# Attention: the second batch of score maxima moved between the first four and the last two value tiles of a group

## The chip, the cores and the metric

The kernel runs on one core of one Trainium2 chip. The metric is the device time of one execution in microseconds; three executions of the kernel before are at hand.

## What is computed

One transformer layer over 2048 latent tokens with 256 context tokens as a prefix. The change touches attention alone:

```python
def attend(q, k, v):
    s = jnp.einsum('bkgqd,bknd->bkgqn', q, k, preferred_element_type=jnp.float32)
    p = jax.nn.softmax(s, axis=-1).astype(v.dtype)
    return jnp.einsum('bkgqn,bknd->bkgqd', p, v)
```

There are 8 query heads of 64 channels on 2 key heads, and 2048 + 256 = 2304 keys, that is 18 key tiles of 128. Everything is float32. The rest of the layer (projections, a gated MLP branch, the merge, a feed-forward network) comes before and behind it.

## The kernel before

Attention (`attend`, L1121) goes through 16 **units**. A unit (class `Unit`, L1993) is one block of 512 queries for two heads. It works in the transposed form: a score tile has 128 keys on the partitions and 512 queries along a row, so the softmax maximum of a query must be known before the scores are exponentiated. It is found in a separate pass, ahead of time, for a later unit:

- `maxima(n)` (L2022) takes the next n steps of 18. A step is two matmuls of 64 rows (one for each head, in the two halves of the array) into two PSUM banks, and two reductions on VectorE (DVE) out of them (L2048; the two steps on the context keys use L2043).
- `reference()` (L2052) joins a unit's maxima, `leading()` (L2059) transposes them and puts them by DMA into one row of the second score operand, so that the second score matmul subtracts them.

The unit itself handles its 18 key tiles in three **groups** of six (`GROUP`). For every tile, `first(j)` (L2077) and `second(j)` (L2087) issue two score matmuls each (L2082 and L2101) into two banks, and ScalarE (ACT) exponentiates both (L2105) into an SBUF tile. `values(j)` (L2108) multiplies the exponentials with the values (L2115); those of a group run one group later, from the list `pend`. A value tile is four matmul instructions of 64 columns, in two pairs. `values` also adds the exponentials of one tile to a running total for the softmax sums: on DVE for tiles 4, 8 and 14 (tile 2 only starts that total; L2128), on GpSimd (POOL) for the others (L2131). `leave()` (L2135) copies the finished output of a unit from its bank (ACT, L2138) and stores it by a DMA that ACT issues; it stands at the end of `pend` for the third group.

So TensorE's order in a group is: 24 score matmuls, a first batch of three maxima steps (6 matmuls; 10 instructions where the context keys are in it), 24 value matmuls of the group before, a second batch of three maxima steps. In the third group the two sums of an older unit (`sums`, L2153: L2157 on TensorE, the copy L2163 and two DMA issues on ACT) follow the values. In the first two groups the maxima are those of the next unit, in the third group those of the one after. At the end of the middle group `reference` of the next unit and `join` (L2141, DVE) of the unit before run, at the end of the third `remainder` (L2017, DVE). In units 1 to 4 a piece of `mod_part` (L355) runs at the fifth tile of a group: two DVE operations on weights and, now and then, a matmul.

All of this shares the eight PSUM banks (tag "b", L1122). One of them holds a unit's output from its first value tile, in the middle group, until `leave` has copied it. The exponentials lie in 8 buffers "p2" (tiles 0 to 3 of a group) and 8 buffers "t4" (tiles 4 and 5).

What sets the order: within `attend`, TensorE and DVE run in the order in which the program is written, because `attend` notes its range in `fixed` (L1170) and `order` (L1867) chains those two engines; new tiles of one tag are also first written in program order on every engine:

```python
            held = idx in pinned or (idx in fixed and i.engine in engines)
            held = held or (idx in loads and i.engine == self.nc.sync.engine)
            after = keys + ([i.engine] if held else [])
```

ACT, POOL and the DMA queue are ordered by the framework's scheduler.

Of the kernel before, what the change touches and what calls it, by code (L numbers as in the profile page):

```python
# [63 lines left out]
}  # L64
SLOTS = {tag: n for tags in POOLS.values() for tag, n in tags.items()}
GROUP = 6
ON_VECTOR = (2, 4, 8, 14)
LAST_ON_VECTOR = (2, 4, 7, 8, 9, 13, 14, 15)


class Kern:
# [1048 lines left out]
    def attend(self, units, late, mod):  # L1120
        self.psum({"b": 8})  # L1121
        begin = self.here()  # L1122
        pend = []
        for i, u in enumerate(units):
            at = lambda n: units[n] if 0 <= n < len(units) else None
            nxt, far, old, older = at(i + 1), at(i + 2), at(i - 1), at(i - 2)
            for gi, g in enumerate(range(0, NKT, GROUP)):
                group = range(g, g + GROUP)
                step = nxt if gi < 2 else far
                for j in group:  # L1130
                    u.first(j)
                    u.second(j)
                    if j % GROUP == 2 and far and gi == 0:
                        far.load()
                    if j % GROUP == 4 and nxt and gi == 2:
                        nxt.leading()
                    if not nxt:
                        next(late, None)
                    elif i and j % GROUP == 4:
                        next(mod, None)  # L1140
                if step:
                    step.maxima(3)
                for f in pend:
                    f()
                if gi == 1 and far:
                    far.cast()
                if gi == 2 and old:
                    old.sums()
                if step:
                    step.maxima(3)  # L1150
                if gi == 0:
                    if older:
                        older.inverse()
                if gi == 2 and far:
                    far.remainder()
                if gi == 1:
                    if nxt:
                        nxt.reference()
                    if old:
                        old.join()  # L1160
                pend = [lambda u=u, j=j: u.values(j) for j in group]
            pend.append(u.leave)
        for _ in mod:
            pass
        for f in pend:
            f()
        units[-2].inverse()
        units[-1].join([self.sb("raw", [TB]) for _ in range(2)])
        self.fixed.append(range(begin, self.here()))
# [823 lines left out]
class Unit:  # L1993
# [93 lines left out]
    def second(self, j):  # L2087
        k = self.k
        c, _, ks = self.keys(j)
        if j % GROUP < GROUP - 2:  # L2090
            whole = k.sb("p2", [2, TB])
# [16 lines left out]
    def values(self, j):  # L2108
# [5 lines left out]
        for h in range(2):  # L2114
# [3 lines left out]
            )  # L2118
        e = j in (LAST_ON_VECTOR if self.last else ON_VECTOR)
        old = self.acc.get(e)  # L2120
# [102 lines left out]
```

## Time and profile before

| | us |
|---|---|
| median of 3 executions | 3059.85 |
| lowest and highest | 3059.34 and 3066.04 |
| span of the profiled execution, first to last instruction | 3053.4 |
| first score block of unit 0 and last values of unit 15 start at | 755.9 and 1408.7 |
| a unit in the middle of the stage (unit 7: 1044.8 to 1085.7) | 40.85 |

The profile is of one execution. Its own time is known as the span; the median of the executions is 6.45 us above that, which lies ahead of the first and behind the last instruction. PE is TensorE's matmuls, PEld its weight loads, DVE VectorE, ACT ScalarE, POOL GpSimd; a q behind a name (ACTq) is an engine's sequencer, which issues DMAs. In rows of the timeline the columns are the start, the length, engine, line, operation, tile names as output<-input, and in square brackets the idle time before the first instruction of the row and what ended it. A row joins several instructions (x6). Matmuls are pipelined, so a row's length is more than its share of the engine's time: the time that a block of matmuls costs is the distance from its start to the start of the next block.

### The profile page before, as it was taken

What the parts mean: (1) busy time and instruction counts of PE and PEld (TensorE: products, weight loads), DVE (VectorE), ACT (ScalarE), POOL (GpSimd) and SP (SyncE); (2) the same over time, 40 slices, a digit from 0 to 9 for tenths busy, and PEclk for the clock granted to TensorE, in tenths of its full rate; (3) what the DMA queues carried; (4) which work ended last, traced back from release to release, by engine and by line L of the source; (5) the groups of instructions that cost most, each with busy time, mean ns of one, the idle gap of its engine ahead of it and who ended that gap; (6) DMA issues with size and microseconds to landing.
All of it is one profiled execution on the core that took longest, in us unless ns stands there. A gap on an engine that the chain in (4) does not pass through costs nothing. (4 is left out here: it accounts for less than half of the span.)

```text
span 3053.4 us, 37883 instructions
## 1 busy us (share of the span) xinstructions
PE 2960.3 (97%) x13325; PEld 2232.3 (73%) x13325; DVE 2093.8 (69%) x3006; ACT 1438.3 (47%) x2334; POOL 659.8 (22%) x472
## 2 busy tenths in 40 slices
PE   7989999999999999998999989999999999999999
PEld 4878788876555555555888878888787888888887
DVE  4866577885898787786655587776676666654555
ACT  5645765563454554544322255444454344444442
POOL 0000000000898889885212200000000000000000
PEclk9999999999999999999999999999999999999999
DMA  8676666654111000004767558888766544447554
GB/s 298 212 253 202 209 199 217 192 172 150 34 42 43 22 22 18 22 19 158 233 204 218 180 172 317 310 301 299 256 216 224 193 149 154 152 149 279 208 212 145
DMA packets 385439, 538.59 MB, mean 176 GB/s; under 512 B 37904, under 2 KB 196800, under 8 KB 385248
## 3 DMA queue, kind: packets, MB, share of 16 engines
q1 hardware_dynamic: 373168, 515.96, 50.8%
q10 hardware_dynamic: 12080, 20.21, 1.8%
q8 instruction: 105, 1.72, 0.2%
q14 instruction: 86, 0.70, 0.1%
HBM read 371.89 MB, written 164.10 MB: 176 GB/s over the span
## 5 line engine op out<-in xcount | busy, mean ns | idle before, releaser
L2048 DVE TENSOR_REDUCE ts<-b 128x1 f32<-128x512 f32 x512 | 314.9, 682 | 94.2 <-PE b L2037 93.9
L2131 POOL TENSOR_TENSOR ac<-ac,p 128x512 f32<-128x512 f32 x216 | 301.7, 1429 | 54.8 <-ACT p L2105 54.8
L1669 DVE TENSOR_TENSOR b<-b,b 128x1024 fp32r<-128x1024 f32 x170 | 200.8, 1221 | 131.1 <-ACT b L1668 130.7
L1668 ACT CAST b<-b 128x1024 fp32r<-128x1024 f32 x170 | 170.6, 1051 | 225.6 <-PE b L1555 106.6
L2105 ACT ACTIVATE p<-b 128x512 f32<-128x512 f32 x384 | 197.5, 611 | 158.1 <-PE b L2101 78.8
L1554 PE MATMUL b<-b,b 128*128 128x512 f32 x680 | 266.2, 391 | 5.6 <-DVE b L1669 5.6
L1553 PE MATMUL b<-b,b 128*128 128x512 f32 x680 | 267.0, 393 | 3.8 <-ACT b L1668 2.4
L1555 PE MATMUL b<-b,b 128*128 128x512 f32 x680 | 265.4, 390 | 0.0
L2131 POOL TENSOR_TENSOR ac<-ac,t 128x512 f32<-128x512 f32 x152 | 221.4, 1485 | 0.0
L2131 POOL TENSOR_TENSOR ac<-p,p 128x512 f32<-128x512 f32 x32 | 47.9, 1518 | 770.3 <-ACT p L2105 770.3
L2082 PE MATMUL b<-h,h 128*128 128x512 f32 x576 | 202.2, 420 | 1.4 <-DVE ts L2048 1.0
L2101 PE MATMUL b<-h,h 128*128 128x512 f32 x576 | 180.8, 395 | 0.0
L2115 PE MATMUL b<-p,h 128*64 128x512 f32 x768 | 175.3, 598 | 1.0 <-ACT p L2105 1.0
L1554 PE MATMUL b<-hb,b 128*128 128x512 f32 x446 | 173.8, 390 | 0.0
L1563 DVE TENSOR_TENSOR f<-f,b 128x512 f32<-128x512 f32 x160 | 109.2, 683 | 78.9 <-issue 46.2
L1553 PE MATMUL b<-hb,b 128*128 128x512 f32 x415 | 161.9, 390 | 0.1
L1555 PE MATMUL b<-hb,b 128*128 128x512 f32 x415 | 161.3, 389 | 0.0
L1554 PEld LDWEIGHTS b<-b,b 128*128 128x128 f32 x680 | 128.1, 188 | 35.6 <-DVE b L1669 8.7
L2082 PEld LDWEIGHTS b<-h,h 128*128 128x128 f32 x576 | 106.9, 190 | 62.6 <-DVE ts L2048 23.2
L1553 PEld LDWEIGHTS b<-b,b 128*128 128x128 f32 x680 | 128.0, 188 | 33.1 <-ACT b L1668 4.2
L1555 PEld LDWEIGHTS b<-b,b 128*128 128x128 f32 x680 | 127.9, 188 | 26.2
L1553 PE MATMUL a<-f,h 128*128 128x384 f32 (+1 forms) x320 | 119.0, 376 | 12.1 <-ACT a L650 4.9
(429 smaller groups left out, 7267.7 us busy)
## 6 DMA issues: line engine op xcount, KB each, us to landing
ao_d<-f SPq DMA_DIRECT2D x224, 256.0 KB
f<-in_w_ff SPq DMA_DIRECT2D x48, 1024.0 KB
b<-ao_d SPq DMA_DIRECT2D x85, 512.0 KB
b<-w2o_d SPq DMA_DIRECT2D x85, 512.0 KB
w2o_d<-f SPq DMA_DIRECT2D x112, 256.0 KB
f<-in_w_in SPq DMA_DIRECT2D x44, 512.0 KB
f<-x_d SPq DMA_DIRECT2D x64, 256.0 KB
hb<-ao_d SPq DMA_DIRECT2D x54, 256.0 KB
```

Of the source, the lines that this page charges most:

```text
L1553: mm(ps, wh, hh, start=start and k == 0, stop=False, skip_group_check=True)
L1554: mm(ps, wh, hl, start=False, stop=False, skip_group_check=True)
L1555: mm(ps, wl, hh, start=False, stop=k == len(w) - 1, skip_group_check=True)
L1563: nc.vector.tensor_tensor(out=out, in0=in0, in1=in1, op=op)
L1668: nc.scalar.copy(h, f32(l))
L1669: nc.vector.tensor_tensor(out=l, in0=f32(l), in1=f32(h), op=ALU.subtract)
L2048: nc.vector.tensor_reduce(out=self.mx[:, t, h, c : c + 1], in_=ps[h], axis=AX.X, op=ALU.max)
L2082: self.nc.tensor.matmul(self.pts[j][h], k.KA[c][self.kv][:, ks], self.qa[h], start=True, stop=False, skip_group_check=True,)
L2101: self.nc.tensor.matmul(s, k.KB[c][self.kv][:, ks], self.qb[h], start=False, stop=True, skip_group_check=True,)
L2105: self.nc.scalar.activation(pt[h], s, AF.Exp)
L2115: nc.tensor.matmul(self.o[h * HD : (h + 1) * HD, :], k.V[c][:, i, self.kv * HD : (self.kv + 1) * HD], pt[h], start=j == 0, stop=j == NKT - 1,)
L2131: nc.gpsimd.tensor_tensor(out=self.acc[e][:, h], in0=old[:, h], in1=pt[h], op=ALU.add)
```

## The change

The pending values of a group are no longer issued as one block. The second batch of maxima goes between the values of the first four tiles and those of the last two. `leave` is no longer an entry of its own in the list; it is called behind the last `values`, so that the last two entries are two value tiles. The calls that stood between the values and the second batch (`far.cast`, `old.sums`) now stand behind it. The numbers and sizes of all operations stay as they are.

```diff
@@ -64,6 +64,7 @@
 GROUP = 6
+LATE = 2
@@ -1140,14 +1141,16 @@
                 if step:
                     step.maxima(3)
-                for f in pend:
+                for f in pend[:-LATE]:
+                    f()
+                if step:
+                    step.maxima(3)
+                for f in pend[-LATE:]:
                     f()
                 if gi == 1 and far:
                     far.cast()
                 if gi == 2 and old:
                     old.sums()
-                if step:
-                    step.maxima(3)
                 if gi == 0:
@@ -1159,7 +1162,7 @@
                 pend = [lambda u=u, j=j: u.values(j) for j in group]
-            pend.append(u.leave)
+            pend[-1] = lambda u=u, f=pend[-1]: (f(), u.leave())
```

## The prediction, made before the change was run

> **What bounds the kernel now.** I read the page's first line, then the busy times by window for the attention stage (after the length: busy us and instruction count of PE, PEld, DVE, ACT, POOL), the waits of TensorE's weight loads there (total us, times, longest), and the timeline of one unit.
>
> ```profile
> PE 2960.3 (97%) x13325; PEld 2232.3 (73%) x13325; DVE 2093.8 (69%) x3006; ACT 1438.3 (47%) x2334; POOL 659.8 (22%) x472
> 755.00:1410.00 655.00, 652.24 (x2968) 348.22 (x2967) 531.68 (x677) 328.50 (x657) 581.25 (x407) 0.99 0.10 30
> PEld b L2082 <- DVE ts L2048: 20.9, 64, 0.7
> ```
>
> TensorE is the bound. In the 655 us of attention it is busy 652.24 us, DVE 531.68, ACT 328.50, POOL 581.25. Busy counts modelled ends, so the question is how closely its instructions start one behind another. Scores (L2082) wait 20.9 us for DVE's maxima (L2048): the banks into which they go are still being reduced. That is what the change can win. Now one unit on TensorE; a row's first column is its start.
>
> ```profile
> 1002.10 1.03 PE L2157 MATMUL b<-ac,ones 128*64 128x512 f32 x4
> 1003.05 0.97 PE L2037 MATMUL b<-h,h 64*128 64x512 f32 x6
> 1003.95 0.88 PE L2082 MATMUL b<-h,h 128*128 128x512 f32 x2
> ...
> 1010.08 1.34 PE L2037 MATMUL b<-h,h 64*128 64x512 f32 x6
> 1011.35 3.65 PE L2115 MATMUL b<-p,h 128*64 128x512 f32 x16
> ...
> 1016.65 0.96 PE L2037 MATMUL b<-h,h 64*128 64x512 f32 x6
> 1017.54 0.74 PE L2082 MATMUL b<-h,h 128*128 128x512 f32 x2
> ...
> 1023.20 0.96 PE L2037 MATMUL b<-h,h 64*128 64x512 f32 x6
> 1024.15 3.65 PE L2115 MATMUL b<-p,h 128*64 128x512 f32 x16
> ...
> 1029.45 0.96 PE L2037 MATMUL b<-h,h 64*128 64x512 f32 x6
> 1030.34 0.88 PE L2082 MATMUL b<-h,h 128*128 128x512 f32 x2
> ...
> 1036.61 1.23 PE L2037 MATMUL b<-h,h 64*128 64x256 f32 x10
> 1037.76 3.65 PE L2115 MATMUL b<-p,h 128*64 128x512 f32 x16
> ```
>
> Differences of starts give the blocks. Scores to first batch: first group 6.13, middle 5.66, last 6.27. First batch: 1.27, 0.95, 1.15. Values: 5.30. Second batch: 0.89. The middle group's 5.66 is the scores block without a DVE wait. The last group also holds a transpose (L2063), an estimated 0.12 (a quarter of a 5.66/12 pair), so its wait is worth 6.27 - 5.66 - 0.12 = 0.49, the first group's 0.47.
>
> **The change, part by part.** Nothing is added or dropped; TensorE and DVE take the new order as written (the hold at L1881). The second batch now runs after 8 of the 12 pairs of value matmuls; 43 groups have both a second batch and pending values (14 first, 15 middle, 14 last groups).
>
> *The extra break, +6.0 us.* One values block becomes two.
>
> ```profile
> 1011.83 0.14 PEld L2115 LDWEIGHTS b<-p,h 128*64 128x64 f32 x2 [0.29 <-issue]
> 1012.26 0.14 PEld L2115 LDWEIGHTS b<-p,h 128*64 128x64 f32 x2 [0.29 <-issue]
> ...
> 1029.45 0.53 PEld L2037 LDWEIGHTS b<-h,h 64*128 64x128 f32 x6 [0.81 <-DVE ac L2128]
> ```
>
> ```profile
> 1375.96 3.65 PE L2115 MATMUL b<-p,h 128*64 128x512 f32 x16
> ...
> 1381.27 0.73 PE L2082 MATMUL b<-h,h 128*128 128x512 f32 x2
> ```
>
> A pair takes 0.43 (1011.83 to 1012.26 in the loads), 12 take 5.16, the block 5.30: 0.14 is fixed per block. Where scores follow values directly, in the last unit, it is again 5.31 (1375.96 to 1381.27), so the new neighbour costs nothing of its own. 43 x 0.14 = 6.0. Lower bound 43 x 0.04 = 1.7 (if only a block's slow first pairs, 3.48 for eight, were paid again). Upper bound: the idle of the weight loads at a break, 0.81 in place of 0.29, all unhidden, 43 x 0.52 = 22; the starts contradict that, so I stay with 0.14. The Trainium skill, page "TensorEngine Tiling (Array Packing)", section "Tiling Modes", says that changing the tiling mode drains TensorE; this speaks against the change, and the 0.14 agrees. The Trainium skill's page "TensorE: Matmul & The Clock Gate", section "Step-by-step: what each phase is for", has about 128 cycles for a drain; at that page's 2.4 GHz this is an estimated 0.053 us a break, by which the sum below would be 3.7 us lower.
>
> *What the DVE waits are really worth.* After the change 1.86 us of values (4 x 0.43 + 0.14) stand between the second batch and the scores, so DVE has that much more time. Next in line are the exponentials on ACT.
>
> ```profile
> 1003.20 0.59 ACT L2163 COPY t<-b 128x512 f32<-128x512 f32 x1 [6.30 <-PE b L2157]
> 1003.82 0.53 ACTq L2166 DMA_DIRECT2D sm_d<-t  x2
> 1005.16 4.24 ACT L2105 ACTIVATE p<-b 128x512 f32<-128x512 f32 x8 [1.37 <-PE b L2101]
> 1009.23 2.13 ACT L2105 ACTIVATE t<-b 128x512 f32<-128x512 f32 x4
> ...
> 1017.38 0.35 ACTq L2139 DMA_DIRECT2D at_d<-t  x1
> 1018.60 4.03 ACT L2105 ACTIVATE p<-b 128x512 f32<-128x512 f32 x8 [1.25 <-PE b L2101]
> 1022.43 2.15 ACT L2105 ACTIVATE t<-b 128x512 f32<-128x512 f32 x4
> ```
>
> ```profile
> 1010.92 0.18 PEld L2037 LDWEIGHTS b<-h,h 64*128 64x128 f32 x1 [0.31 <-ACT t L2105]
> ```
>
> The first group's last maxima load (1010.92) waits for the eleventh exponential, that is for its bank. So the first group is set by ACT at its end, not by the DVE waits ahead of it. Unhindered, ACT starts 1.06 after the scores (1018.60 - 1017.54), takes 3.83 for eight (1022.43 - 1018.60) and ends the eleventh 5.46 after its first. The waits delay it as well: start 1.21, eight in 4.07.
>
> First group: the sums' matmuls now end just ahead of the scores instead of a batch earlier, so their copy and DMA issues fall into the scores. Today the copy starts 0.15 into the block that follows the sums (1003.20 - 1003.05); that block will be the scores. 0.15, 0.59 of copy, 0.03, 0.53 of issues: 1.30. In the last unit, where this order stands already, an exponential follows its issue so:
>
> ```profile
> 1371.84 0.53 ACTq L2166 DMA_DIRECT2D sm_d<-t  x2
> 1372.46 4.03 ACT L2105 ACTIVATE p<-b 128x512 f32<-128x512 f32 x8
> ```
>
> 0.09 behind the issue's end, so ACT starts at 1.40 instead of 1.21. Scores to values: 1.40 + 5.46 + 0.09 (wake) + 0.43 (load to next block) = 7.38, against 7.40 now. The whole 0.47 is gone: 13 x -0.02 = -0.3. In unit 1, with no sums ahead, start 1.06 gives 7.04: -0.35. Bounds for the 13: -0.34 each (issue out of the way) to +0.15.
>
> Middle group: the output's copy and issue (0.35) likewise move into the scores; issue ends at 0.11 + 0.58 + 0.04 + 0.35 = 1.08, ACT starts near 1.18 instead of 1.06. With one bank more in rotation (the output's is free) this reaches the maxima by 0.05: 11 x 0.05 = +0.55.
>
> Last group: no sums or output copy in front, so ACT starts at 1.06 instead of 1.22 and runs at full pace.
>
> ```profile
> 1023.73 3.68 DVE L2048 TENSOR_REDUCE ts<-b 128x1 f32<-128x512 f32 x6 [2.87 <-PE b L2037]
> 1027.33 1.78 DVE L2128 TENSOR_TENSOR ac<-p,t 128x1024 f32<-128x1024 f32 x1
> 1029.98 3.68 DVE L2048 TENSOR_REDUCE ts<-b 128x1 f32<-128x512 f32 x6 [0.86 <-PE b L2037]
> ```
>
> ```profile
> 1031.56 4.18 ACT L2105 ACTIVATE p<-b 128x512 f32<-128x512 f32 x8 [6.97 <-POOL ac L2131]
> 1035.60 1.12 ACT L2105 ACTIVATE t<-b 128x512 f32<-128x512 f32 x2
> ...
> 1036.70 1.06 ACT L2105 ACTIVATE t<-b 128x512 f32<-128x512 f32 x2
> ```
>
> The eleventh exponential ends about 1.66 behind the ninth's start (1035.60 to half of 1036.70's pair, a small copy between), so at 1.06 + 3.83 + 1.66 = 6.55; with the first group's 0.09 and 0.43 the values start at 7.07, against 7.42 now (1037.76 - 1030.34): 15 x -0.35 = -5.2. TensorE alone would reach 6.93, all of the 0.49. One thing can eat this. The add for key tile 4 (L2128, 1.78) is among the last two values, so DVE now runs it behind the second batch. From the start of the middle group's first batch: second batch at 0.95 + 3.58 = 4.53, its reduces 5.06 to 8.66, add until 10.44. The last group's scores start at 4.53 + 0.89 + 1.86 = 7.28, and its third key tile wants a buffer at 7.28 + 1.06 + 4 x 0.479 = 10.26, the fourth at 11.2. Buffer numbers are left out of the rows. Tile 2's buffer, which that add holds, comes free last of its four; I take it that the fourth gets it, and no wait. If the third does, 0.24 of each 0.35 is lost: -1.6 in place of -5.2. The reference and the join behind the add reach 12.0, ahead of the next batch's reduces at 13.6; queued behind that add they delay no one.
>
> Units 1 to 4, where DVE also scales weights:
>
> ```profile
> 803.39 3.65 PE L2115 MATMUL b<-p,h 128*64 128x512 f32 x16
> ...
> 816.25 0.96 PE L2037 MATMUL b<-h,h 64*128 64x512 f32 x6
> ```
>
> ```profile
> 805.65 3.67 DVE L2048 TENSOR_REDUCE ts<-b 128x1 f32<-128x512 f32 x6
> ```
>
> The earlier batch would start at 803.39 + 3.58 = 806.97, but its sixth bank comes with the fifth reduce of the first batch, at 805.65 + 3.07 = 808.72. The batch itself stalls; the values go on at 809.2, end at 811.1, and the scores, 5.7 long, at 816.8 instead of 816.25. That is 0.5, of which 0.14 is counted: 4 x 0.36 = +1.4.
>
> Sum: 6.0 - 0.3 - 0.35 + 0.55 - 5.2 + 1.4 = **+2.1 us**. POOL (581.25 of 655) keeps its order; SP's loads and the stage behind attention move along, TensorE staying the bound. The profiled span is 3053.4; the median of the runs, 3059.85, is 6.45 more, around the span, and the change does not touch that. 3059.85 + 2.1 = 3062.
>
> **The rivals.** *Faster: the waits are PE time, and ACT is not in the way.* If banks were the only limit, all goes: 15 x 0.49 + 14 x 0.47 = 13.9, less 6.0: -8 us, 3052. For it: 20.9 us of waits, the middle group runs at 5.66. Against: the 0.31 wait at 1010.92, and that ACT needs 0.479 an exponential (3.83/8) where TensorE needs 0.47 for its two matmuls (5.66/12). Chance 0.22.
>
> *Slower: the output's bank.* In the middle group the scores follow the leave copy's start instead of its end. If the second score matmul is given the output's bank, it waits from 0.25 until 0.69 plus a wake, 0.5 us, and ACT with it: 15 x 0.5 = 7.5 on top of 2.1, 3069.5. It decides as soon as that bank is among the first two taken; from the fifth on it costs nothing. For it: the output is held until that copy. Against: one spare bank and DVE's first reduce are free earlier. The 3.6 us of tile 2's buffer and a first group at its +0.15 (2.2 more than counted) would end near it too, at 3068. Chance together 0.35.
>
> That the order does not change at all is excluded by the hold on TensorE and DVE.
>
> **How the numbers follow.** A measurement of this kernel tells about 0.2%, 6.1 us, from no change: below 3053.7 is faster, above 3066.0 slower. Forecast 0.43 (its own range 3054 to 3066), faster rival 0.22, slower 0.35. The range reaches into both: 3050 to 3072.
>
> **What would show it.** Right: value blocks of 3.58 and 1.86 with a batch between; almost no wait of L2082 for L2048; the first group's scores to values still near 7.4, with ACT's first exponential about 1.4 behind the scores; the last group's 7.42 down to 7.1. Wrong: a first group near 7.05 (faster), or a middle group over 6.7 with scores waiting for ACT's L2138 (slower), a third exponential of the last group waiting for L2128, or a break dearer than 0.14.

## The result, and the profile after

The changed kernel takes 3062.84 us (median of 13 runs, 3058.91 to 3069.53), the kernel before beside it 3062.5 (13 runs). The ratio is 1.0009, with a 95% interval of 1.0001 to 1.0016: 2.8 us slower, between 0.3 and 4.9 (the two medians alone differ by 0.3). The forecast was 3062.0, 2.1 us slower. The profiled span is 3058.7, 5.3 more than before. So the number came out; the profile shows that several of the steps behind it did not.

Attention by window, columns as in the prediction (length; busy us and count of PE, PEld, DVE, ACT, POOL; clock; DMA share; GB/s):

```profile
755.00:1413.00 658.00, 641.23 (x2928) 343.61 (x2929) 515.75 (x676) 323.90 (x656) 569.49 (x403) 0.99 0.10 30
```

TensorE is still the bound, but it is idle 16.8 us here (658.00 - 641.23) where it was idle 2.8 (655.00 - 652.24). The waits of its weight loads name the place (780 to 1362 us; total, times, longest):

```profile
PEld b L2085 <- DVE ts L2051: 34.6, 44, 0.8
PEld b L2040 <- issue: 26.1, 40, 0.8
PEld b L2040 <- DVE ts L2051: 25.0, 25, 2.4
PEld b L2040 <- ACT t L2108: 7.5, 27, 0.4
PEld b L2118 <- DVE ts L2051: 7.2, 14, 0.6
```

The first row is a trap. 44 waits of 0.8, 34.6 us, look like more waiting for DVE than before (some 21 us), but the scores follow the short values block now, and 0.81 is what the weight loads idle at any break behind values (the 0.81 in the prediction's row at 1029.45, where another line was named). The scores start on time. The third and fifth rows are new (before, 3.2 us in 4 waits, and none): the *batch itself* (L2040) and the values behind it (L2118) wait for reductions. One unit on TensorE, unit 7:

```profile
1050.30 0.73 PE L2085 MATMUL b<-h,h 128*128 128x512 f32 x2
...
1055.98 0.73 PE L2040 MATMUL b<-h,h 64*128 64x512 f32 x3
1057.26 0.73 PE L2040 MATMUL b<-h,h 64*128 64x512 f32 x3 [0.55 <-DVE ts L2051]
1057.92 3.65 PE L2118 MATMUL b<-p,h 128*64 128x512 f32 x16
1061.51 0.96 PE L2040 MATMUL b<-h,h 64*128 64x512 f32 x6
1062.40 1.94 PE L2118 MATMUL b<-t,h 128*64 128x512 f32 x8
1064.27 0.73 PE L2085 MATMUL b<-h,h 128*128 128x512 f32 x2
...
1071.21 3.65 PE L2118 MATMUL b<-p,h 128*64 128x512 f32 x16 [0.20 <-DVE ts L2051]
...
1077.55 0.73 PE L2085 MATMUL b<-h,h 128*128 128x512 f32 x2
...
1084.60 3.65 PE L2118 MATMUL b<-p,h 128*64 128x512 f32 x16
```

Blocks, start to start: values 3.59 and 1.87, as forecast. Scores to values: first group 7.62 (1050.30 to 1057.92; forecast 7.38), middle 6.94 (forecast 6.66), last 7.05 (forecast 7.07). The first batch of the first group is torn in two: three matmuls at 1055.98, three at 1057.26. The weight loads show for whom the second half waits, and VectorE's rows show which reductions there were:

```profile
1057.26 0.30 PEld L2040 LDWEIGHTS b<-h,h 64*128 64x128 f32 x3 [0.98 <-DVE ts L2051]
```

```profile
1056.51 3.68 DVE L2051 TENSOR_REDUCE ts<-b 128x1 f32<-128x512 f32 x6 [2.61 <-PE b L2040]
...
1070.47 3.68 DVE L2051 TENSOR_REDUCE ts<-b 128x1 f32<-128x512 f32 x6 [4.58 <-PE b L2040]
```

DVE had been idle for 2.61 us when its first reduction of this very batch began at 1056.51, so no older reduction was left to wait for: the fourth matmul waits until that one has ended (its load starts at 1057.26), and that means that it was given a bank which the batch itself had just filled. In the middle group the six matmuls of the batch run through (from 1069.94), but the values behind it wait in the same way: DVE had been idle for 4.58, and the first matmul into the output's bank (1071.21) follows the end of the batch's first reduction. The trace has no bank numbers; which bank it is cannot be read from it. ScalarE does what the prediction said:

```profile
1050.44 0.59 ACT L2166 COPY t<-b 128x512 f32<-128x512 f32 x1 [7.33 <-PE b L2160]
1051.06 0.53 ACTq L2169 DMA_DIRECT2D sm_d<-t  x2
1051.68 4.03 ACT L2108 ACTIVATE p<-b 128x512 f32<-128x512 f32 x8 [0.66 <-POOL ac L2134]
...
1065.46 4.03 ACT L2108 ACTIVATE p<-b 128x512 f32<-128x512 f32 x8 [0.48 <-PE b L2104]
...
1078.61 4.03 ACT L2108 ACTIVATE p<-b 128x512 f32<-128x512 f32 x8 [7.17 <-PE b L2104]
```

The first exponential is 1.38 behind the scores in the first group, 1.19 in the middle, 1.06 in the last; forecast 1.40, 1.18, 1.06.

Where the 5.3 us of span came from, by landmarks of the two traces (PE rows):

| stretch | before | after | difference |
|---|---|---|---|
| ahead of unit 0's scores | 755.88 | 756.69 | +0.81 |
| units 0 to 4 | 207.21 | 210.54 | +3.33 |
| units 5 to 14 | 406.85 | 412.91 | +6.06 |
| unit 15, first scores to last values' start | 35.31 | 36.96 | +1.65 |
| last values' start to the merge's first matmul | 12.31 | 7.07 | -5.24 |
| the rest | 1635.84 | 1634.53 | -1.31 |

Attention lost 11 us, and the seam behind it gave 5 back. Not all of the 5.3 is the change. In the runs that have both on record, the time is 1.8 to 2.2 us above the span, and not 6.45; by this the profiled execution of the kernel before took an estimated 3055.5, 4.3 less than the median of the three, and most of the 6.45 does not lie around the span. Unit 15 repeats badly too: in e3 below, whose attention has the same code as the kernel before, it takes 36.46. (Last values are the whole block of six tiles, from 1405.25 before.) The seam, before (ACT's queue, SP's queue and PE):

```profile
1411.25 0.35 ACTq L2139 DMA_DIRECT2D at_d<-t  x1
1413.33 0.39 SPq L1229 DMA_DIRECT2D bw<-in_w_br_attn  x1
1417.56 0.79 PE L183 MATMUL b<-in,bw 128*128 128x512 f32 x1 [6.99 <-ACT bw L150]
```

and after:

```profile
1417.96 0.53 ACTq L2169 DMA_DIRECT2D sm_d<-t  x2
1419.52 0.39 SPq L1232 DMA_DIRECT2D bw<-in_w_br_attn  x1
1424.17 0.50 PE L184 MATMUL b<-in,bw 128*128 128x512 f32 x1 [1.75 <-ACT bw L151]
```

What SP waited for ahead of that load (us in total, times, longest), before and after:

```profile
SPq L1229 <- DMA at_d<-t: 28.6, 1, 28.6
```

```profile
SPq L1232 <- DMA sm_d<-t: 22.8, 1, 22.8
```

The merge's first weight load (bw) goes to memory that a buffer of attention leaves. Before, that is the buffer from which the last output is stored (at_d<-t), the last thing that attention does; after, it is that of the last sums (sm_d<-t), which are stored ahead of the last values. The load comes 2.1 and 1.6 us behind the issue of the store that frees its memory, and in the new order that store is earlier.

### The profile page after: what moved, and what is told of

It reads as the page before. It is cut to its first block, busy times and chain, and to the rows that moved or that the text cites. A ratio compares the mean times of both kernels' runs of the same rounds, so it can differ in the third digit from the quotient of the medians.

```text
span 3058.7 us, 37898 instructions
## 1 busy us (share of the span) xinstructions
PE 2956.2 (97%) x13325; PEld 2228.6 (73%) x13325; DVE 2084.8 (68%) x3006; ACT 1434.2 (47%) x2334; POOL 655.2 (21%) x472
## 4 chain that ended last, share of the span: by engine, by line
PE 81%; DVE 7%; DMA 6%; ACT 2%; issue 2%; SPq 1%; ACTq 0%; POOL 0%; DVEq 0%; POOLq 0%
PE b L1557 14%; PE b L1556 14%; PE b L1558 13%; PE b L2118 8%; PE b L2085 4%; PE b L184 4%; PE b L186 4%; PE b L185 4%; PE b L2104 4%; PE a L1556 3%; PE a L1557 3%; PE a L1558 3%; PE b L2040 3%; DVE ts L2051 2%; PE b L190 1%
## 5 line engine op out<-in xcount | busy, mean ns | idle before, releaser
L2134 POOL TENSOR_TENSOR ac<-ac,t 128x512 f32<-128x512 f32 x152 | 214.9, 1442 | 0.0
L2085 PE MATMUL b<-h,h 128*128 128x512 f32 x576 | 187.1, 406 | 0.8 <-DVE ts L2051 0.4
L2104 PE MATMUL b<-h,h 128*128 128x512 f32 x576 | 179.6, 393 | 2.1 <-DMA h<-t 2.1
L2118 PE MATMUL b<-p,h 128*64 128x512 f32 x768 | 177.0, 603 | 3.4 <-DVE ts L2051 2.7
```

What stands on the lines that cost most here:

```text
L2085: self.nc.tensor.matmul(self.pts[j][h], k.KA[c][self.kv][:, ks], self.qa[h], start=True, stop=False, skip_group_check=True,)
L2104: self.nc.tensor.matmul(s, k.KB[c][self.kv][:, ks], self.qb[h], start=False, stop=True, skip_group_check=True,)
L2118: nc.tensor.matmul(self.o[h * HD : (h + 1) * HD, :], k.V[c][:, i, self.kv * HD : (self.kv + 1) * HD], pt[h], start=j == 0, stop=j == NKT - 1,)
L2134: nc.gpsimd.tensor_tensor(out=self.acc[e][:, h], in0=old[:, h], in1=pt[h], op=ALU.add)
```

## The experiments

The theory after the comparison: (1) the break and the last group are as forecast; (2) the framework's choice of banks, which the new order changed, costs the first and middle groups some 0.5 us a unit and more in units 0 to 4; (3) the copy of the sums, now behind the scores, sets the first group; (4) the end gain is the reused buffer alone. Rivals stand in the expectations. Each kernel ran beside the kernel before; "units 5 to 14" is the stretch that repeats best (406.85 and 406.88 in two kernels with the same code there), "unit 15 and seam" goes from unit 15's first scores to the merge's first matmul. The median of the kernel before, beside these, lay between 3059.16 and 3062.5, so ratios are compared and not medians.

| kernel | median us (runs) | ratio, 95% interval | units 5 to 14 | unit 15 and seam |
|---|---|---|---|---|
| before (profile) | 3059.85 (3) | 1 | 406.85 | 47.62 |
| changed | 3062.84 (13) | 1.0009, 1.0001 to 1.0016 | 412.91 | 44.03 |
| e1 changed, banks in turn | 3055.21 (11) | 0.9985, 0.9976 to 0.9994 | 408.46 | 45.00 |
| e2 before, banks in turn | 3075.38 (5) | 1.0053, 1.0039 to 1.0067 | 415.37 | 48.26 |
| e3 before, spare buffer | 3051.56 (11) | 0.9979, 0.9971 to 0.9988 | 406.88 | 43.59 |
| e4 middle only, in turn | 3066.17 (7) | 1.0024, 1.0013 to 1.0035 | 410.55 | 50.27 |
| e5 middle only, spare | 3049.69 (5) | 0.9964, 0.995 to 0.9978 | 404.69 | 44.03 |
| e6 sums first, in turn, spare | 3051.16 (5) | 0.9968, 0.9956 to 0.9981 | 404.92 | 44.20 |
| e7 the same, no spare | 3055.33 (11) | 0.9985, 0.9976 to 0.9994 | 404.96 | 49.51 |
| e8 changed, row first | 3066.71 (9) | 1.0026, 1.0016 to 1.0036 | 413.10 | 44.49 |
| e9 e5, row first | 3050.94 (6) | 0.9967, 0.9956 to 0.9979 | 404.73 | 45.94 |
| e10 e8 once more | 3068.64 (1) | one execution | 413.04 | 47.17 |

**e1, the banks.** The changed kernel, but attention hands out its eight banks strictly in turn; the output's is out of the round until it has been copied.

```diff
     def bank(self, shape, dtype=F32, tag="b"):
+        if self.ring is not None:
+            tag = self.ring.pop(0)
+            self.ring.append(tag)
+            self.latest = tag
...
-        self.psum({"b": 8})
+        self.ring = [f"b{n}" for n in range(8)]
+        self.psum({tag: 1 for tag in self.ring})
...
             self.o = k.bank([TB])
+            self.held = k.latest
+            k.ring.remove(self.held)
...
         self.nc.scalar.copy(oc, self.o)
+        k.ring.append(self.held)
```

> The changed kernel, but the eight banks of attention are handed out strictly in turn (the longest free one first, the output's bank taken out while it is held). Theory 'bank choice': in the changed kernel the first group's fourth maxima matmul gets the bank of the same batch's first step, and the middle group's output gets such a bank too; both then wait for DVE's first reduce. In turn, these waits go: scores to values 7.62 -> 7.38 in the first group and 6.95 -> 6.66 in the middle one, 0.5 us a unit, about 7 us less than the changed kernel, ratio to before about 0.9985. Rival 'exponentials': those two blocks end with ACT whatever bank is used; then 7.6 and 6.9 stay and the ratio stays at 1.001.

Confirmed. In e1's unit 7, whose scores begin at 1048.09, no batch is torn:

```profile
1053.77 1.77 PE L2048 MATMUL b<-h,h 64*128 64x512 f32 x6
1055.46 3.65 PE L2128 MATMUL b<-p,h 128*64 128x512 f32 x16
```

Scores to values are 7.37 here (7.38 in the median of the units), what the prediction had worked out; the middle group's is 6.72. The batch's waits for reductions, 25.0 us in the changed kernel, are all but gone (780 to 1362 us):

```profile
PEld b L2048 <- DVE ts L2059: 0.7, 2, 0.4
```

Units 5 to 14 lose 4.45 of the 6.06, and units 1 to 4 take 166.24 against 172.14 in the changed kernel and 167.10 before.

**e2, the same in the order before.**

> The kernel before with the same banks in turn, the control for the first run. If the choice of banks in the kernel before was already harmless, scores to values stay at 7.40, 6.61 and 7.41 and the ratio is 1.000 within 0.001. If banks in turn are better in themselves, this run gains as much as the first one and the first says nothing on the change.

A miss: 0.5% slower. "In turn" is not neutral. With the scores right behind the second batch, they soon come to the banks that this batch has just filled, and wait for its reductions; the free choice had done better. The waits of e2's score loads for DVE (780 to 1362 us; total, times, longest) are twice those of the kernel before, where the same stretch has 66 waits and 21.5 us:

```profile
PEld b L2090 <- DVE ts L2056: 42.9, 120, 0.8
```

The middle group's scores take 6.09 instead of 5.66. So the change does remove a wait: under in-turn banks it is worth 415.37 - 408.46 = 6.9 us in ten units. The free choice of the kernel before, at 406.85, lost 8.5 us less than banks in turn in the same order.

**e3, the seam alone.** The kernel before; the last unit takes one more output buffer ahead of its own and sets one element of it, so that the merge's load lies over another.

```diff
+        if self.last:
+            for _ in range(1):
+                spare = k.t2([TB])
+                self.nc.vector.memset(spare[:1, :1], 0.0)
         oc = k.t2([TB])
```

> The kernel before; in the last unit only, one more small buffer of the kind 't2' is taken (and one element of it set) ahead of the output's copy, so that the first weight load of the merge stage no longer lies over the buffer from which the last output is stored. Theory: in the kernel before SP's first load of bw waits for that store (issued at 1411.25, load at 1413.33), and the changed kernel escaped this by chance, which gave it back about 5 us of what attention lost. Then the gap between the start of the last values and the merge's first matmul falls from 12.3 - 5.3 us behind to about 7, and the ratio is 0.9984 (-5 us). Rival: the gap is set by POOL's last adds and the join; then it stays and the ratio is 1.000.

Confirmed: last values to the merge's first matmul 7.12 instead of 12.31, units 5 to 14 as before (406.88), 0.21% faster.

**e4, one part of the change.** Only the middle group's second batch is moved; banks in turn as in e2.

```diff
-                for f in pend[:-LATE]:
+                late_n = LATE if gi == 1 else 0
+                for f in pend[: len(pend) - late_n]:
                     f()
+                if gi == 2 and old:
+                    old.sums()
                 if step:
                     step.maxima(3)
-                for f in pend[-LATE:]:
+                for f in pend[len(pend) - late_n :]:
                     f()
...
```

> Of the change, only the middle group's second batch is moved (the one ahead of the last group's scores); the first and last groups keep the old order, so that neither the sums' copy nor the output's copy comes between values and scores. Banks in turn. By the terms of the prediction: a middle group +0.14 (second break), a last group -0.35 (DVE's wait gone, exponentials the limit), first group unchanged, in all -0.2 a unit or -3 us against the kernel before with banks in turn; ratio 0.999. Rival 'a break costs more than 0.14 or the waits are hidden anyway': no gain, ratio 1.000 or above.

Against e2, units 5 to 14 lose 4.8 us: each middle group pays its break (values 3.58 + 1.87 for 5.30) and each last group behind it falls from 14.74 to 14.11, more than the 0.35 forecast because in-turn banks had made it wait longer. Its number missed: 1.0024 came where 0.999 was expected, because that ratio took banks in turn to be neutral, which e2 refutes.

**e5, the best part with the best seam.** The middle group's move, free choice of banks, e3's spare buffer.

> The kernel before with the second batch moved in the middle group alone, the framework's own bank choice, and one spare output buffer taken at the last unit. Theory: a middle group's move costs its break (0.15) and gives 0.35 in the last group behind it, so a unit is 40.65 us against 40.86 (13.60 + 12.95 + 14.10), 15 units -3 us; the end of attention gives a further 6.4 us: -9 us in all, ratio 0.997. Rival: the middle group alone gains nothing because the moved add or a bank eats it (last group still near 14.4): 0.998, the spare buffer's share alone. Rival: the batch's banks are reused here as well (middle group at 13.3): 0.9985.

Confirmed: 12.95 + 14.11 + 13.59 = 40.65 a unit, against 40.86; 404.69 against e3's 406.88 in ten units. No first batch is torn here: in units 5 to 14 it takes at most 1.31 us in the first and 1.16 in the middle group (1.30 and 1.16 in the kernel before). The ratio is the lowest of the study, 0.36% below the kernel before; e6 and e9 lie inside its interval.

**e6 and e7, the copy of the sums.** The changed kernel with banks in turn, and the sums ahead of the third group's second batch; e6 with e3's spare buffer, e7 without.

```diff
                 for f in pend[:-LATE]:
                     f()
+                if gi == 2 and old:
+                    old.sums()
                 if step:
                     step.maxima(3)
...
-                if gi == 2 and old:
-                    old.sums()
```

> The changed kernel with banks in turn, the softmax sums of the third group issued ahead of the second batch, and the spare output buffer. Theory: in the first group the copy of the sums and its two DMA issues on ScalarE, which the change put behind the scores, are what sets 7.38 us from scores to values; with the sums ahead of the batch, ScalarE starts 1.06 behind the scores and the distance is 7.05, 13 groups -4.3 us against the version in turn with the sums behind: ratio 0.997. Rival: DVE or a bank sets it and the distance stays at 7.38: 0.9985.

> The same without the spare buffer, so that the merge's first weight load lies over the buffer from which the last output is stored. Theory: the end of attention (last values to the merge's first matmul) is 12.3 us instead of 7.1, so 5 to 6 us slower than with the spare buffer: ratio 0.999. Rival: with the new order of the last group the load is not what the merge waits for, and both versions take the same time: 0.997.

Both confirmed. In e6's unit 7, whose scores begin at 1045.79, the first batch and the values behind it, then ScalarE:

```profile
1051.46 1.44 PE L2048 MATMUL b<-h,h 64*128 64x512 f32 x6
1052.83 3.65 PE L2128 MATMUL b<-p,h 128*64 128x512 f32 x16
```

```profile
1043.17 0.59 ACT L2181 COPY t<-b 128x512 f32<-128x512 f32 x1 [4.57 <-PE b L2175]
...
1046.85 4.03 ACT L2116 ACTIVATE p<-b 128x512 f32<-128x512 f32 x8 [3.09 <-PE b L2112]
```

The copy is out of the way, the first exponential follows the scores by 1.06, and scores to values are 7.04 instead of e1's 7.38: 0.34 a group, 3.5 us over units 5 to 14 (408.46 to 404.92). e7 differs from e6 by the seam alone, 49.51 against 44.20.

**e8 to e10, the last unit.** Its second score matmul waits for the row of maxima (h<-t) in the changed kernel, because SP's queue issued another load ahead of the eight DMAs; before, it was the other way round (L2068 at 1364.01, L1199 at 1369.05). The two rows of SP and that of the weight load:

```profile
1376.96 0.35 SPq L1202 DMA_DIRECT2D raw<-gm_d  x1
1377.41 4.93 SPq L2071 DMA_DIRECT2D h<-t  x8
```

```profile
1383.44 0.19 PEld L2104 LDWEIGHTS b<-h,h 128*128 128x128 f32 x1 [2.23 <-DMA h<-t]
```

e8 holds SP to the written order for these two; e9 does so in e5.

```diff
+        at = self.here()
         ahead = fetch(*items[0])
+        if b == 0:
+            self.loads.append(range(at, self.here()))
...
+        at = k.here()
...
+        if self.last:
+            k.loads.append(range(at, k.here()))
```

> The changed kernel with one order added on SyncE's queue: the eight DMAs that put the last unit's maxima into the score operand (h<-t) are issued ahead of the first load for the stage behind attention (raw<-gm_d), as they are in the kernel before. Theory: the last unit's first group of scores takes 6.0 to 6.2 us instead of 8.29, and the last values start 2.2 us earlier; ratio to the kernel before 1.0002 (1.0009 less 0.0007). Rival: the row of maxima itself comes late in the new order, or something else waits next, and the block stays above 7.5: 1.0009.

> The kernel with the middle group's move alone and the spare output buffer, with the same order on SyncE's queue. Theory: the last unit's first scores take 6.1 us instead of 8.30, 2.2 us less: ratio 0.9957 against 0.9964 without it. Rival: the later load for the stage behind attention costs there what it saves here: 0.9964.

The block did what it should, the time did not. The last unit's first scores take 6.31 (e8) and 6.58 (e9) instead of 8.29 and 8.30, and its second scores then 8.79 and 9.35 instead of 6.34 and 6.32: the rival of e9 is right, and e8's "something waits next" too, but one group later than the block it named. e8 was also slower ahead of that, and its profile holds one odd add (below). e10 is a second profile of e8:

> The kernel of the run before last once more, for a second profile of it. In its first profile one add on VectorE in unit 1 took 6.62 us where it takes 1.61 in the changed kernel's, while GpSimd ran four adds. If that belongs to the program, the last group of unit 1 shows scores of 9.3 us again; if it belonged to that one execution, 5.8.

The add was ordinary again (scores 5.80). The last unit was not: first scores 6.19, second 9.60, and the values behind them 7.27 instead of 5.30. ACT and the weight load in e10:

```profile
1399.53 0.62 ACT L151 CAST in<-raw 128x512 fp32r<-128x512 f32 x1 [2.94 <-DVE raw L1224]
1400.06 1.56 ACT L2114 ACTIVATE p<-b 128x512 f32<-128x512 f32 x3
```

```profile
1400.70 0.29 PEld L2091 LDWEIGHTS b<-h,h 128*128 128x128 f32 x1 [3.13 <-ACT p L2114]
```

ACT's order has casts for the next stage between the exponentials. Their inputs are loaded later now, and the exponentials queued behind a cast wait with it. Part of the loss is the clock: it is 0.50 from 1400 to 1406 us, while the values, 7.27 long, begin. Saved 2.1, lost 3.3 and 2.0: unit 15 and the seam go from 44.03 to 44.49 (e8) and 47.17 (e10).

## Why the prediction was right, and where not

**The extra break: right.** Forecast 0.14, measured 0.15 to 0.16 (3.59 + 1.87 against 5.30), 43 times 6.5 us. The 0.053 that the prediction worked out beside it from the Trainium skill's page "TensorE: Matmul & The Clock Gate", section "Step-by-step: what each phase is for", is a third of that.

**The last group: right.** 7.05 against 7.07 forecast and 7.42 before. No exponential waits for the moved add (the eight in 4.03 at 1078.61). Which key tile gets its buffer, the trace does not show, and it did not matter:

```profile
1078.93 1.21 DVE L2131 TENSOR_TENSOR ac<-p,t 128x1024 f32<-128x1024 f32 x1
```

The add took 1.21 instead of 1.78 and ended at 1080.14, ahead of the third tile's first exponential at 1080.53.

**The first group: the step "scores to values 7.38 against 7.40 now" failed, by its last link.** ACT starts at 1.38, as forecast, and e1 gives 7.38 when no bank is used twice in a batch. In the changed kernel it is 7.62: the batch waits for its own first reduction. The prediction asked which bank comes free when, and took for granted that a bank that is free gets used.

**The middle group: +0.05 forecast, +0.33 measured (6.94 against 6.61).** The same cause; 6.72 in e1. That the output's bank is free by then was no help. (The prediction counts 11 such groups; the output's copy falls into 14, units 1 to 14, which is 0.15 us more.)

**Units 0 to 4.** The prediction's terms for them come to some +1.3 (14 breaks 1.96, DVE's weights 1.4, less 1.75 for the last groups and 0.35 for unit 1); the traces differ by 3.3. Unit 0 blurs this: it takes 40.11 in the kernel before and 38.39 in e3, which have the same code in it, and the granted clock is 0.50 from 768 to 771 us in the one and 1.00 in the other. Units 1 to 4 alone repeat: 167.10 and 167.12 (before and e3), 172.14 and 172.13 (changed and e10). The change costs 5.0 us there. The stalls expected there did appear, but the large ones in other places: the first batch of units 2 and 4 takes 3.30 and 3.32 instead of 1.27, because its own first reduction, for which it waits, stands behind DVE's weights. Behind unit 2's stall the clock falls as well (last section), and the 16 value matmuls take 5.28 instead of 3.58. In e1 the two batches take 1.6 and the values 3.58.

**"SP's loads and the stage behind attention move along": failed twice.** The seam gave back 5.2 us (e3, e6 and e7 show that the buffer's place alone does this), and unit 15, where SP's new order makes the scores wait 2.2 us, takes 1.65 longer; against e3, with the old code and 36.46, it is 0.5, so how much of this is the change is not shown.

So 11 us were lost where 2.1 were forecast, and 5.2 came back from a place that was called unchanged: the predicted time was right in part by luck, because two errors cancelled.

**The rivals.** *Faster* needed a first group near 7.05; it stayed behind ACT, and e6 shows that the copy of the sums was the reason. *Slower* named the right resource, a bank handed out before it was free, and the wrong taker: not the scores behind the output's copy, but the batch and the output themselves.

**What stays open.** The changed kernel was not run with the spare buffer alone, so that its seam was set by the sums' store rests on SP's wait. How much of unit 15's 1.65 us is the change. And a version in which neither the row of maxima nor the next stage's loads are late in the last unit was not found.

## What to carry to other kernels

A new order of the work is also a new assignment of buffers: look in the trace for a batch that waits for its own first result, and ask at the end of each stage whose memory the next stage's first load takes. Here these two effects, -5 us at the seam and some +7 for the banks (the ratios of the changed kernel and e1, 1.0009 and 0.9985), were each as large as the change's intended parts (+6.5 and -5). The shortest way to the gain was to keep the one part of the change that paid (the middle group's move, 0.2 us a unit) and to take the seam's 5 us by a buffer that nobody else needs.

## What the runs showed of the hardware

**An idle of 7 us, and at times one of 2 us, halves the clock for what follows.** The granted clock (third from the right) in the four microseconds around and behind the merge's first matmul, before:

```profile
1417.00:1421.00 4.00, 3.44 (x8) 2.73 (x9) 1.29 (x2) 1.02 (x2) 0.00 (x0) 0.50 1.00 308
```

and after:

```profile
1424.00:1428.00 4.00, 3.83 (x15) 2.85 (x16) 1.29 (x2) 0.96 (x3) 0.00 (x0) 1.00 0.94 297
```

Behind an idle of 6.99 it is 0.50, and the first 13 matmuls take 5.7 us (1417.56 to 1423.27); behind 1.75 it is 1.00, and they take 3.4 (1424.17 to 1427.58). The seam's wait thus costs some 2.3 us more than its length at first. In unit 2 of the changed kernel it is 0.50 behind an idle of 1.92:

```profile
845.04 0.72 PE L2040 MATMUL b<-h,h 64*128 64x512 f32 x3 [1.92 <-DVE ts L2051]
```

```profile
846.00:849.00 3.00, 3.00 (x10) 0.83 (x8) 3.00 (x5) 0.00 (x0) 3.00 (x3) 0.50 0.15 55
```

In unit 4 the same stall (idle 1.95) leaves it at 1.00, and e10 shows the same pair, 1.94 with and 1.92 without. The Trainium skill's page "TensorE: Matmul & The Clock Gate", section "What's actually happening", has half the clock after an idle window of about 3.4 us and full clock after as long a busy one. The seam's two values agree with the idle's side of it, unit 2's 1.92 us does not, and the measurement decides; the return to full speed took 5.7 us at the seam.

**One add on VectorE lasted as long as four on GpSimd.** In e8's unit 1, DVE and then POOL:

```profile
823.35 6.62 DVE L2137 TENSOR_TENSOR ac<-p,t 128x1024 f32<-128x1024 f32 x1
```

```profile
823.90 4.98 POOL L2140 TENSOR_TENSOR ac<-ac,p 128x512 f32<-128x512 f32 x4
```

In the changed kernel's profile the same add took 1.61. It ends 1.1 us behind the fourth of GpSimd's adds, and the last group's scores took 9.35 in place of 5.82. The Trainium skill's page "SBUF — State Buffer", section "SBUF: two separate sides", has a pair of ports that VectorE with two inputs and GpSimd lock against each other for a whole instruction. That would explain it, but here VectorE would have stood aside for four instructions in a row, not one. It is not shown to be the cause, and it happened in this one execution; e10, with the same program, has the ordinary add.
